# Two unused tiles that shift the matmul operands of a hybrid DeltaNet / mLSTM layer to multiples of 512 bytes

## The chip, the cores and the metric

The kernel runs on one core of one Trainium2 chip. The metric is the time of one execution on the device, in microseconds (us); the median of several runs counts. The core has a tensor engine (TensorE: matmuls, whose stationary operand is loaded beforehand and whose moving operand streams past it), VectorE, ScalarE, GpSimd (POOL) and 16 DMA engines. Work on different engines overlaps as far as data allow. On-chip memory has 128 partitions; a tile occupies the same byte range in each of them, so a tile has one start address, counted in bytes from the beginning of a partition.

## What is computed

One layer of a bidirectional backbone on 128 context tokens and 256 latent tokens, width 2048, all in float32. The two blocks below run once for the context and once for the latents; `mod` comes from `silu(cond) @ w_ada + b_ada`.

```python
def block(x, mod, init_states, lp, grid):
    ...
    shift1, scale1, gate1, shift2, scale2, gate2 = jnp.split(mod, 6, axis=-1)
    h = rmsnorm(x, pre1) * (1.0 + scale1) + shift1
    mix, states = mixer(h, grid, init_states, w_in, conv_w, a_log, dt_bias, norm_a, ibias, fbias, norm_b, w_out)
    x = x + gate1 * rmsnorm(mix, post1)
    h = rmsnorm(x, pre2) * (1.0 + scale2) + shift2
    f = jnp.square(jax.nn.relu(h @ w1)) @ w2
    x = x + gate2 * rmsnorm(f, post2)
    return x, states
```

`mixer` projects `h` with `w_in` (2048 x 7216), runs a gated delta rule (8 heads) and an mLSTM (4 heads) forward and backward in chunks, and projects the joined heads with `w_out` (2048 x 2048). The feed-forward part has a hidden width of 8192.

## The kernel before

All 384 tokens (three tiles of 128) are worked on together. Every large product has a right-hand side of weights from HBM. A weight block of two k-tiles (128 x 2 x 512 floats, 512 KB) lands in a tile `raw`; ScalarE rounds it to the reduced float format that TensorE takes at full rate (`whi`, line 332) and VectorE computes what is left (`wlo`, line 333). The activations are held in two such parts as well, so that each product is done as three: high by low, high by high, low by high. `gemm` writes these triples in two forms. With `fm` true (lines 356 to 358), the weights are stationary and 384 tokens move: the projections of q, k and v and the up projection of the feed-forward part. With `fm` false (lines 360 to 362), 128 tokens are stationary and 512 weight columns move: the projections of the mLSTM values and gates, the output projection (`mid`, activations `y`) and the down projection (`ffn`, activations `ah` and `al`). For the last weight blocks of the output and of the down projection (`room`), the weights are held in tiles of their own (`w_ah`, `w_al`, and `w` in the memory of `h`).

The order of the stages is: set-up and `phase1` (normed input, modulation, mLSTM projections), the mLSTM heads, four quarters of the delta rule (whose own small products stand between the triples of the next projection), the output projection with residual and second norm (`mid`), the feed-forward part (`ffn`: eight chunks, the up projection of one ahead of the down projection of the one before), and the last norm. Steps of the modulation (`ps_ada`, line 190, and `adav` on VectorE, line 220) are put between the large products by `fill`. Each engine takes its instructions in the order in which they are written, with some parts moved forward by a priority.

Tiles are allocated in pools, and pools that live at the same time lie behind one another: first `cp` (constants), then `hp` (activation operands `h`, `y`), `wp` (`raw`, `whi`, `wlo`), `wk` (small work tiles), and behind these the pools of the stage, of which `fp` is the one of `mid` and `ffn`. A tile's start is therefore the sum of what lies ahead of it. In the built program, all tiles of `hp` and `wp` begin at 160 bytes past a multiple of 512, and the large ones of `fp` at 480 past one. Slices that the products take (a k-tile of 1536 or 2048 bytes, a block of 128 columns of 512 bytes) keep that remainder.

Of the kernel before, what the change touches and what calls it, by code (L numbers as in the profile page):

```python
# [12 lines left out]
F32 = mybir.dt.float32  # L13
# [8 lines left out]
P = 128  # L22
# [114 lines left out]


def ada_mod(S, sec, k0, m, pv):
    """Bias of the modulation columns pv [P, m, 2], and what each section is used as: shift, scale or gate."""  # L140
    nc, c = S.nc, S.c
    i = sec // 3
    cols = lambda t, o: t[:, o + k0:o + k0 + m].unsqueeze(2).to_broadcast([P, m, 2])
    bias = cols(c.pcol, 16 * sec)
    if sec % 3 == 0:
        nc.vector.tensor_tensor(c.tcol[i][:, k0:k0 + m, :], pv, bias, op=ALU.add)
        return
    tmp = S.wk.tile([P, m, 2], F32, tag="adatmp", name="adatmp")
    nc.vector.tensor_tensor(tmp, pv, bias, op=ALU.add)
    if sec % 3 == 1:  # L150
        nc.vector.scalar_tensor_tensor(c.scol[i][:, k0:k0 + m, :], in0=tmp, scalar=1.0, in1=cols(c.pcol, 96 + 16 * i),
                                       op0=ALU.add, op1=ALU.mult)
    else:
        nc.vector.tensor_tensor(c.gcol[i][:, :, k0:k0 + m].rearrange("p v k -> p k v"), tmp,
                                cols(c.pcol, P + 16 * i), op=ALU.mult)


def ada_cols(S, ps, n):
    """Four groups of 32 rows of sums, n wide, turned into columns: [P, group, block, row of the group]."""
    nc = S.nc  # L160
    row = S.wk.tile([P, 256], F32, tag="modrow", name="modrow", bufs=1)
    nc.scalar.copy(row[:, 0:n], ps[:, 0:n])
    pt = S.pa.tile([P, 512], F32, tag="a", name="ps_col")
    for i in range(n // P):
        nc.tensor.transpose(pt[:, i * P:i * P + P], row[:, i * P:i * P + P], S.c.ident)
    t = S.wk.tile([P, 4, n // P, 2], F32, tag="modcol", name="modcol")
    nc.vector.tensor_copy(t, pt[:, 0:n].rearrange("p (i j r) -> p j i r", j=4, r=32)[:, :, :, 0:2])
    return t


def ada_steps(S, units, n):
    """Blocks of n columns of silu(cond) @ w_ada + b_ada, units (section, first column), brought to columns; one step
    at a time, to go between the steps of a larger product. Four products at a time, each on its own 32 columns of
    the tensor engine: the units, and as many k-tiles as there is room for."""
    nc, c = S.nc, S.c
    nu = len(units)
    npar = 4 // nu
    kn = 1024 // (nu * n)
    ps = S.pa.tile([P, 512], F32, tag="a", name="ps_ada")
    for k in range(0, NK, kn):  # L180
        raw = S.wp.tile([P, kn, nu * n], F32, tag="raw", name="raw_ada", bufs=S.nraw)
        runs = [(0, nu)] if nu == 4 else [(u, u + 1) for u in range(nu)]
        for u, e in runs:
            o = units[u][0] * D + units[u][1]
            nc.sync.dma_start(raw[:, :, u * n:e * n], S.A.w_ada[0, k * P:(k + kn) * P, o:o + (e - u) * n]
                              .rearrange("(k p) n -> p k n", p=P))
        for kk in range(kn):
            for u in range(nu):
                j = u * npar + (k + kk) % npar
                nc.tensor.matmul(ps[32 * j:32 * j + 32, 0:n], lhsT=c.scz[:, k + kk, :],  # L190
                                 rhs=raw[:, kk, u * n:u * n + n], start=k + kk < npar, stop=k + kk >= NK - npar)
        yield
    t = ada_cols(S, ps, n)
    m = n // P
    if npar == 1:
        ada_mod(S, units[0][0], units[0][1] // P, 4 * m, t.rearrange("p j i v -> p (j i) v"))
        return
    for u, (sec, c0) in enumerate(units):
        s = S.wk.tile([P, m, 2], F32, tag="modsum", name="modsum")
        nc.vector.tensor_tensor(s, t[:, 2 * u], t[:, 2 * u + 1], op=ALU.add)  # L200
        ada_mod(S, sec, c0 // P, m, s)


def ada_vec(S, sec, c0):
    """The same for 512 columns of a section, summed over the k-tiles by the vector engine."""
    nc, c = S.nc, S.c
    while S.av is None:
        yield
# [24 lines left out]


def fill(S, n=None):
    """Some steps of the work that waits to go between the steps of the products."""
    if n is None:
        S.credit += S.rate
        n = int(S.credit)
# [13 lines left out]


def ada_later(S, sec, nvec=0):
    """A section by halves of 1024 columns on the tensor engine, the last nvec by the vector engine."""
    for i in range(2):
        if i < 2 - nvec:
            S.todo.append(ada_steps(S, [(sec, 1024 * i + 256 * u) for u in range(4)], 256))
# [7 lines left out]


def gate_rows(S, i):
    """gate * post-norm weight as rows in DRAM, to be broadcast over the tokens."""  # L270
    nc, c = S.nc, S.c
    ps = S.pa.tile([P, 512], F32, tag="a", name="ps_gr")
    nc.tensor.transpose(ps[0:32, 0:P], c.gcol[i].rearrange("p v k -> p (v k)"), c.ident)
# [12 lines left out]


def build_hT(S, xs, kt, which, diag=None):
    """h^T of one 128-feature block (all tokens), split in two float32r parts."""
    nc, c = S.nc, S.c  # L290
    ps = S.pm.tile([P, 512], F32, tag="m", name="ps_hT")
    for t in range(NT):
# [12 lines left out]


def diag_of(S, r, t):
    """diag(r): transposes and scales rows in one product."""
    d = S.wk.tile([P, P], F32, tag="diag", name="diag", bufs=3)
    S.nc.vector.tensor_scalar(d, S.c.ident, r, None, op0=ALU.mult)  # L310
    return d


def alloc_act(S):
    """Two halves of an activation operand [2048, 384] as float32r pairs."""
    hh = [[S.hp.tile([P, 8, TOK], F32R, tag=f"h{a}{b}", name=f"h{a}{b}") for b in range(2)] for a in range(2)]
    return lambda kt: (hh[kt // 8][0][:, kt % 8, :], hh[kt // 8][1][:, kt % 8, :])


def wchunk(S, srcs, kn, dst=None):  # L320
    """kn k-tiles of a block of weights, side by side from srcs, as a float32r pair whose sum is exact."""
    nc = S.nc
    n = sum(ap.shape[1] for ap in srcs)
    raw = S.wp.tile([P, kn, n], F32, tag="raw", name="raw", bufs=S.nraw)
# [10 lines left out]


def gemm(S, fm, wsrc, kcs, act, evac, psum=None, kn=2, between=None, room=()):
    """A block of act^T W over chunks kcs of kn k-tiles; fm: features on partitions, otherwise tokens. With room for
    the weights of the last chunks, these are held and multiplied with one tile of tokens after the other, so that
    what follows a tile need not wait for the rest."""  # L340
    nc = S.nc
    psum = psum or (lambda s: S.pg.tile([P, 512], F32, tag="g", name="ps_g"))
    ps = [None] * 4
# [41 lines left out]


def phase1(S):
    """x, modulation and the mLSTM projections, by quarters of the contraction."""
    nc, tc, A, c = S.nc, S.tc, S.A, S.c
    S.hT = alloc_act(S)  # L390
    S.bqk = [S.mp.tile([P, 2, TOK], F32, tag=f"bqk{h}", name=f"bqk{h}") for h in range(HB)]
# [74 lines left out]


def setup3(S, p1):
    """The gate columns of w_in, padded to a width that the tensor engine takes in one pass, in two parts."""
    nc, A = S.nc, S.A  # L470
    w = p1.tile([P, NK, GW], F32, name="wg")
    nc.gpsimd.memset(w, 0.0)
# [17 lines left out]


def rows3(S, nat, n, name):
    """n per-token columns as rows over the tokens, each the exact sum of three bfloat16 rows 32 apart: a one-hot
    column then spreads a row over all partitions in one pass."""
    nc = S.nc
    pad = S.ga.tile([P, NT, 80], F32, name=name + "p")
    nc.vector.memset(pad, 0.0)
# [17 lines left out]


def gates(S, gt):
    """Per-token gate scalars of both mixers, tokens on partitions."""
    nc, c, gp = S.nc, S.c, S.gp
    G = S.G = SimpleNamespace()  # L520
    T = lambda n, name: gp.tile([P, NT, n], F32, name=name)
# [227 lines left out]
        nc.gpsimd.memset(t, 0.0)  # L749


# Diagonal 32 x 32 blocks between rows on partitions, [(block, row), unit, col], and blocks on partitions,
# [(block, unit), row, col]: with 13 units, prime to 32, both are one regular walk over the DRAM tile.
NI = 52  # L754
DMA_SCRATCH = 1024
LAY = 32 * 13 * 4 * 32 + 32 * 13 * 32
# [25 lines left out]


def delta_quarter(S, q, sqk, sv):
    """Gated delta rule of heads 2q and 2q + 1, both directions."""
    Q = SimpleNamespace()
    Q.qT = [sqk[:, h, :] for h in range(2)]
    Q.kT = [sqk[:, 2 + h, :] for h in range(2)]
# [82 lines left out]


def delta_sub(S, Q):
    """Inverses of the 32 x 32 diagonal blocks, one block per partition, by forward substitution."""
    nc, dl, Am = S.nc, S.dl, Q.Am
    dA, dX = [S.dr.tile([LAY], F32, tag=f"dA{i}", name=f"dA{i}") for i in range(2)]
    tA, X = S.tA, S.X
# [16 lines left out]


def delta_levels(S, Q):
    """The diagonal blocks joined to the inverse of the whole 128 x 128 triangle."""
    nc, dl, Am, pt, dX = S.nc, S.dl, Q.Am, Q.pt, Q.dX
    Tm, Nc = S.Tm, S.Nc
    Nx = dl.tile([P, 13, 32], F32, tag="Nx", name="Nx", bufs=1)  # L900
# [50 lines left out]


def delta_scan(S, Q, q):
    """The tiles in order, for two heads and two directions in step."""
    nc, c, G = S.nc, S.c, S.G
    kT, col, pt, w, at, qe, nk, sv = Q.kT, Q.col, Q.pt, Q.w, Q.at, Q.qe, Q.nk, Q.sv
    chains = [(d, h) for d in range(2) for h in range(2)]
# [85 lines left out]


def ag_block(S, n):
    """Gates of four delta heads; then the gated, normed outputs, transposed and split."""
    nc, c = S.nc, S.c
    ga = S.de.tile([P, NT, 512], F32, tag="slq", name="ga", bufs=2)

# [15 lines left out]


def mid(S):
    """Output projection, first residual, second norm and modulation."""
    nc, tc, A, c = S.nc, S.tc, S.A, S.c
    S.x1 = [S.fp.tile([P, D], F32, name=f"x1_{t}") for t in range(NT)]  # L1070
    mp = S.fp
# [9 lines left out]
        nc.vector.tensor_tensor(S.x1[s][:, cs], ps, gp1[min(s, 1)][:, cs], op=ALU.mult)  # L1081

    def load(n, i):
        """Rows that the residual needs, between the weights."""
        if i in (4, 5):
            cs = slice(n * 512, n * 512 + 512)
            nc.sync.dma_start(gp1[i - 4][:, cs], S.gpd[0][i - 4][cs].partition_broadcast(P))
# [119 lines left out]
def body(tc, A, O):  # L1207
    with ExitStack() as ctx:
# [10 lines left out]
        S.pg = ent(tc.tile_pool(name="pg", bufs=4, space=PSUM))  # L1219
        S.pm = ent(tc.tile_pool(name="pm", bufs=3, space=PSUM))  # L1220
        S.pa = ent(tc.tile_pool(name="pa", bufs=1, space=PSUM))
        S.gpd = [S.drp.tile([2, D], F32, name=f"gpd{i}") for i in range(2)]
        S.gbd = [S.drp.tile([P, 1024], F32, name=f"gbd{t}") for t in range(NT)]
        with ExitStack() as mx:
# [38 lines left out]
            yA_finish(S, 1, g1)  # L1263
        S.fp = ent(tc.tile_pool(name="fp", bufs=1, reuse_waits="tile"))
        S.av = S.fp
        S.rate = R2
        mid(S)
        S.rate = R3
# [20 lines left out]
```

## Time and profile before

| what | value |
|---|---|
| median of three runs | 2026.45 us (2025.23 to 2031.12) |
| span of the profiled execution (its own time, first to last instruction) | 2022.6 us |
| TensorE busy | 1960.9 us, 97% |
| VectorE busy | 1166.6 us, 58% |
| ScalarE busy | 710.8 us, 35% |
| moved from and to HBM | 166 GB/s over the span |

The profile is one execution. PE stands for TensorE's matmuls, PEld for its loads of stationary operands, which overlap them; DVE is VectorE and ACT is ScalarE. Matmuls are pipelined: a product's duration reaches past the start of the next one, so the pace of a stream of products is the distance from start to start, and not the duration of one. A busy share of 97% says that TensorE seldom waits, and not that it works at its peak.

### The profile page before, as it was taken

The page shows a single profiled execution, that of the slowest core. Times are in us where ns is not written, and L with a number is a line of the kernel's source. Part 1 is how long each engine was busy: PE and PEld are TensorE (multiplying, and loading weights), DVE is VectorE, ACT ScalarE, POOL GpSimd, SP SyncE. Part 2 cuts the span into 40 slices and gives each one's busy share as a digit, 9 for nine tenths or more (in the row PEclk, how much of TensorE's full clock was granted, in tenths as well). Part 3 has the DMA queues.
Part 4 walks back from the last instruction along what each step waited for, and adds up shares of the span by engine and source line. Part 5 has one row for each costly group of instructions (what it writes and reads, how often), then busy time and mean ns, then how long its engine had stood idle before and what let it go on. Part 6 is the DMA issues. An engine that isn't in the chain of part 4 may idle for free.

```text
span 2022.6 us, 28836 instructions
## 1 busy us (share of the span) xinstructions
PE 1960.9 (97%) x11332; PEld 1672.3 (83%) x11332; DVE 1166.6 (58%) x2144; ACT 710.8 (35%) x1125; POOL 123.0 (6%) x125
## 2 busy tenths in 40 slices
PE   6999997999999999998999999999999999999997
PEld 4677886788888777788998897988988989889886
DVE  3766883668878766767554465556543343343445
ACT  5222242444444334335433342332332423323322
POOL 2000000010000000000100010000000100000002
PEclk9999998999999999999999999999999999999999
DMA  9988448776576566762454554555544434444452
GB/s 271 293 265 263 126 127 145 165 190 200 164 196 186 154 197 202 266 205 74 142 161 156 165 158 150 161 155 160 157 135 125 127 126 127 129 126 127 125 167 104
DMA packets 232356, 337.25 MB, mean 167 GB/s; under 512 B 46272, under 2 KB 115584, under 8 KB 231196
## 3 DMA queue, kind: packets, MB, share of 16 engines
q1 hardware_dynamic: 214120, 333.15, 55.1%
q10 hardware_dynamic: 17620, 2.11, 0.7%
q8 instruction: 89, 1.46, 0.3%
q14 instruction: 47, 0.39, 0.1%
q0 software_dynamic: 480, 0.15, 0.0%
HBM read 326.80 MB, written 8.56 MB: 166 GB/s over the span
## 4 chain that ended last, share of the span: by engine, by line
PE 72%; DVE 2%; DMA 1%; ACT 0%; issue 0%; POOL 0%; DVEq 0%; POOLq 0%; ACTq 0%
PE ps_g L356 11%; PE ps_g L358 10%; PE ps_g L357 10%; PE ps_dn L362 9%; PE ps_dn L360 9%; PE ps_dn L361 9%; PE ps_g L360 3%; PE ps_g L362 3%; PE ps_g L361 3%; PE ps_ada L190 2%; PE ps_o L1027 1%; DVE wlo L333 1%; PE ps_z L993 1%; DMA raw_av<-w_ada 1%; PE ps_S L1006 0%; PE ps_ks L984 0%
## 5 line engine op out<-in xcount | busy, mean ns | idle before, releaser
L333 DVE TENSOR_TENSOR wlo<-raw,whi 128x1024 fp32r<-128x1024 f32 (+1 forms) x402 | 487.1, 1212 | 586.8 <-ACT whi L332 585.8
L332 ACT CAST whi<-raw 128x1024 fp32r<-128x1024 f32 (+1 forms) x402 | 416.8, 1037 | 1029.5 <-PE ps_g L357 380.6
L356 PE MATMUL ps_g<-h,whi 128*128 128x384 f32 x1536 | 522.7, 340 | 0.5 <-DVE cv L737 0.5
L358 PE MATMUL ps_g<-h,wlo 128*128 128x384 f32 x1536 | 516.3, 337 | 2.1 <-DVE wlo L333 2.1
L357 PE MATMUL ps_g<-h,whi 128*128 128x384 f32 x1536 | 516.8, 336 | 0.0
L356 PEld LDWEIGHTS ps_g<-h,whi 128*128 128x128 f32 x1536 | 288.8, 188 | 20.7 <-issue 18.6
L362 PE MATMUL ps_dn<-wlo,ah 128*128 128x512 f32 x756 | 298.3, 395 | 1.0 <-DVE wlo L333 1.0
L360 PE MATMUL ps_dn<-whi,al 128*128 128x512 f32 x756 | 298.7, 395 | 0.0
L361 PE MATMUL ps_dn<-whi,ah 128*128 128x512 f32 x756 | 298.4, 395 | 0.0
L358 PEld LDWEIGHTS ps_g<-h,wlo 128*128 128x128 f32 x1536 | 288.5, 188 | 5.0 <-DVE wlo L333 4.0
L357 PEld LDWEIGHTS ps_g<-h,whi 128*128 128x128 f32 x1536 | 288.8, 188 | 1.1 <-issue 0.4
L362 PEld LDWEIGHTS ps_dn<-wlo,ah 128*128 128x128 f32 x756 | 141.6, 187 | 36.5 <-DVE wlo L333 1.8
L360 PEld LDWEIGHTS ps_dn<-whi,al 128*128 128x128 f32 x756 | 141.6, 187 | 36.0 <-issue 1.6
L361 PEld LDWEIGHTS ps_dn<-whi,ah 128*128 128x128 f32 x756 | 141.6, 187 | 34.0
L220 DVE SCALAR_TENSOR_TENSOR adav<-raw_av,scz,adav 128x512 f32<-128x512 f32 x180 | 130.6, 774 | 13.0 <-DMA raw_av<-w_ada 12.8
L1148 POOL TENSOR_TENSOR rl<-rl 128x384 f32<-128x384 f32 x64 | 68.1, 1073 | 886.6 <-ACT ah L1147 886.4
L360 PE MATMUL ps_g<-whi,h 128*128 128x512 f32 x288 | 118.4, 411 | 0.5 <-ACT whi L332 0.4
L361 PE MATMUL ps_g<-whi,h 128*128 128x512 f32 x288 | 114.6, 398 | 0.0
L362 PE MATMUL ps_g<-wlo,h 128*128 128x512 f32 x288 | 113.6, 398 | 0.2 <-DVE wlo L333 0.2
L190 PE MATMUL ps_ada<-raw_ada,scz 128*32 128x256 f32 (+1 forms) x1216 | 102.0, 389 | 5.0 <-DMA raw_ada<-w_ada 3.4
L190 PEld LDWEIGHTS ps_ada<-raw_ada,scz 128*32 128x32 f32 x1216 | 34.1, 113 | 47.7 <-issue 27.4
L360 PEld LDWEIGHTS ps_g<-whi,h 128*128 128x128 f32 x288 | 54.1, 188 | 23.1 <-issue 11.3
(400 smaller groups left out, 1899.1 us busy)
## 6 DMA issues: line engine op xcount, KB each, us to landing
raw<-w_ffn SPq DMA_DIRECT2D x256, 512.0 KB, 3.8
raw_ada<-w_ada SPq DMA_DIRECT2D x80, 512.0 KB, 5.0
raw<-w_in SPq DMA_DIRECT2D x74, 512.0 KB, 4.4
raw_ada<-w_ada SPq DMA_DIRECT2D x128, 256.0 KB, 4.8
raw_av<-w_ada SPq DMA_DIRECT2D x48, 512.0 KB, 4.6
raw<-w_in SPq DMA_DIRECT2D x76, 256.0 KB, 3.1
raw<-w_out SPq DMA_DIRECT2D x32, 512.0 KB, 4.6
x<-x_sample SPq DMA_DIRECT2D x2, 1024.0 KB, 9.8
```

Of the source, the lines that this page charges most:

```text
L190: nc.tensor.matmul(ps[32 * j:32 * j + 32, 0:n], lhsT=c.scz[:, k + kk, :], rhs=raw[:, kk, u * n:u * n + n], start=k + kk < npar, stop=k + k ...
L220: nc.vector.scalar_tensor_tensor(acc[:, v, :], in0=raw[:, kt % 2, :], scalar=w, in1=acc[:, v, :], op0=ALU.mult, op1=ALU.add)
L332: nc.scalar.copy(hi, raw)
L333: nc.vector.tensor_tensor(lo, raw, hi.bitcast(F32), op=ALU.subtract)
L356: nc.tensor.matmul(o, lhsT=hi[:, kk, w], rhs=al, start=st, stop=False)
L357: nc.tensor.matmul(o, lhsT=hi[:, kk, w], rhs=ah, start=False, stop=False)
L358: nc.tensor.matmul(o, lhsT=lo[:, kk, w], rhs=ah, start=False, stop=sp)
L360: nc.tensor.matmul(o, lhsT=al[:, w], rhs=hi[:, kk, :], start=st, stop=False)
L361: nc.tensor.matmul(o, lhsT=ah[:, w], rhs=hi[:, kk, :], start=False, stop=False)
L362: nc.tensor.matmul(o, lhsT=ah[:, w], rhs=lo[:, kk, :], start=False, stop=sp)
L993: nc.tensor.matmul(pz[:, i * P:(i + 1) * P], lhsT=S.Tm[d][:, 3 * h + tof(d), :], rhs=r[d, h], start=True, stop=True)
L1148: nc.gpsimd.tensor_tensor(rl, rl, rl, op=ALU.mult)
```

## The change

Two tiles are allocated that nothing writes or reads: 88 floats (352 bytes of a partition) as the first tile of `cp`, and 48 floats (192 bytes) as the first of `fp`. Besides, the comment lines at the head of some functions are gone.

```diff
@@ body
         S.pa = ent(tc.tile_pool(name="pa", bufs=1, space=PSUM))
+        S.cp.tile([P, 88], F32, name="padc")
         S.gpd = [S.drp.tile([2, D], F32, name=f"gpd{i}") for i in range(2)]
...
         S.av = S.fp
+        S.fp.tile([P, 48], F32, name="padf")
         S.rate = R2
```

The built programs have the same instructions, in the same order on every engine and with the same waits. The starts of the tiles (bytes past a multiple of 512) are:

| pool, tiles | before | after |
|---|---|---|
| `hp`: `h`, `y`, `w` | 160 | 0 |
| `wp`: `raw`, `whi`, `wlo` | 160 | 0 |
| `fp`: `x1`, `y2`, `gp1`, `gp2`, `ah`, `al`, `w_ah`, `w_al` | 480 | 0 |
| `fp`: `rl` / `adav`, `fj` | 128 / 32 | 160 / 64 |
| `mp`: `bqk` / `vaug` | 128 / 128, 160, 192 | 480 / 480, 0, 32 |
| delta rule: `da` / `slq`, `slv`, `cv` / `Am`, `DT`, `qe` / `Tm` | 128 / 0 / 384 / 192 | 480 / 352 / 224 / 32 |
| `p1`: `x`, `bo`, `wgh` | 352, 384, 384 | 192, 224, 224 |

## Rows read from the trace of the kernel before

**Rows 1.** The page's head and busy times: us (share of the span) xinstructions.

```profile
span 2022.6 us, 28836 instructions
...
PE 1960.9 (97%) x11332; PEld 1672.3 (83%) x11332; DVE 1166.6 (58%) x2144; ACT 710.8 (35%) x1125; POOL 123.0 (6%) x125
```

**Rows 2.** Windows by stage, us: busy time of each engine (instructions), granted clock, DMA.

```profile
core 0: us, PE busy (x) PEld busy (x) DVE busy (x) ACT busy (x) POOL busy (x), PEclk, DMA share, GB/s
0.00:120.00 120.00, 100.02 (x717) 70.30 (x721) 66.57 (x145) 42.05 (x64) 14.45 (x27) 1.00 0.92 279
120.00:280.00 160.00, 159.71 (x936) 130.00 (x929) 120.52 (x226) 43.91 (x54) 0.00 (x0) 1.00 0.62 193
280.00:420.00 140.00, 122.04 (x679) 99.71 (x678) 79.30 (x247) 63.93 (x140) 6.19 (x9) 0.94 0.76 150
420.00:770.00 350.00, 347.94 (x2845) 284.62 (x2844) 258.00 (x741) 145.32 (x339) 15.03 (x8) 1.00 0.63 184
770.00:917.00 147.00, 145.73 (x692) 114.50 (x690) 103.83 (x155) 55.24 (x81) 1.10 (x2) 1.00 0.68 226
917.00:930.00 13.00, 5.56 (x25) 4.80 (x25) 9.40 (x22) 9.70 (x15) 2.12 (x4) 0.74 0.24 81
930.00:1068.00 138.00, 137.35 (x806) 136.64 (x806) 81.17 (x111) 53.48 (x76) 14.04 (x14) 1.00 0.46 138
1068.00:2013.00 945.00, 942.54 (x4651) 831.70 (x4650) 443.43 (x494) 296.48 (x360) 69.50 (x62) 1.00 0.46 140
```

**Rows 3.** Waits of TensorE: waiting for whom, us in total, times, longest.

```profile
PE ps_c L94 <- ACT crs L93: 8.5, 1, 8.5
...
PE ps_ada L190 <- DMA raw_ada<-w_ada: 3.4, 3, 2.9
...
PE ps_num L689 <- ACT cf L676: 15.8, 3, 8.0
...
PE ps_hT L295 <- DVE s L1118: 7.0, 1, 7.0
```

**Rows 4.** One line in one up projection, 1677 to 1744 us: durations, first and last start.

```profile
L357 PE MATMUL ps_g<-h,whi x128: 334/334/338, 1677.3 to 1743.4; 128*128 128x384 f32 x128
```

**Rows 5.** Timeline of TensorE in the output projection: start us, duration us.

```profile
859.81 0.39 PE L360 MATMUL ps_g<-whi,y 128*128 128x512 f32 x1
...
861.85 0.39 PE L360 MATMUL ps_g<-whi,y 128*128 128x512 f32 x1
```

**Rows 6.** One line in one down projection, 1744 to 1811 us.

```profile
L361 PE MATMUL ps_dn<-whi,ah x96: 394/394/394, 1744.0 to 1810.5; 128*128 128x512 f32 x96
```

**Rows 7.** A window without other work, and TensorE's timeline in it.

```profile
2000.00:2002.20 2.20, 2.20 (x11) 1.75 (x10) 0.00 (x0) 0.00 (x0) 0.00 (x0) 1.00 0.00 0
...
1999.81 0.39 PE L362 MATMUL ps_dn<-w,ah 128*128 128x512 f32 x1
...
2002.14 0.39 PE L360 MATMUL ps_dn<-whi,al 128*128 128x512 f32 x1
```

**Rows 8.** Plain float32 products of an mLSTM head: timeline, and durations of that line.

```profile
382.45 1.03 PE L689 MATMUL ps_num<-vaug,E 128*128 128x257 f32 x4
...
L689 PE MATMUL ps_num<-vaug,E x8: 377/379/380, 381.6 to 384.0; 128*128 128x257 f32 x8
```

**Rows 9.** Groups by line and shape: count, busy us, mean ns, idle before.

```profile
L356 PE MATMUL ps_g<-h,whi 128*128 128x384 f32 x1536 | 522.7, 340 | 0.5 <-DVE cv L737 0.5
...
L360 PE MATMUL ps_dn<-whi,al 128*128 128x512 f32 x756 | 298.7, 395 | 0.0
...
L360 PE MATMUL ps_g<-whi,h 128*128 128x512 f32 x288 | 118.4, 411 | 0.5 <-ACT whi L332 0.4
L360 PE MATMUL ps_g<-whi,y 128*128 128x512 f32 x180 | 71.4, 397 | 0.0
...
L360 PE MATMUL ps_dn<-w,al 128*128 128x512 f32 x12 | 4.7, 396 | 0.0
L360 PE MATMUL ps_g<-w_ah,y 128*128 128x512 f32 x6 | 2.4, 396 | 0.0
```

**Rows 10.** The same groups: the first of the delta rule's products of 128 columns.

```profile
L1027 PE MATMUL ps_o<-vv,at 128*128 128x128 f32 x96 | 17.6, 278 | 0.0
```

**Rows 11.** The page's groups: the split of the weights.

```profile
L333 DVE TENSOR_TENSOR wlo<-raw,whi 128x1024 fp32r<-128x1024 f32 (+1 forms) x402 | 487.1, 1212 | 586.8 <-ACT whi L332 585.8
L332 ACT CAST whi<-raw 128x1024 fp32r<-128x1024 f32 (+1 forms) x402 | 416.8, 1037 | 1029.5 <-PE ps_g L357 380.6
```

## The prediction

> **What bounds the kernel now.** I read the page's first lines, then the windows by stage, then who waits for whom, and last the spacing of the large products. The profiled execution spans 2022.6 us and TensorE is busy in 1960.9 us of it [rows 1]; the median of the three timed runs is 2026.45 us, so 3.9 us lie around the span and are added to every forecast. By stage TensorE is busy nearly without a gap from 120 us to the end, save the gate and mLSTM stretch (122.0 of 140 us) and the hand-over to the feed-forward part (5.6 of 13 us) [rows 2]. What TensorE waited for is short: 8.5 us for ScalarE at the start, 15.8 us for the mLSTM states, 7.0 us at the hand-over, 3.4 us for weights from DMA [rows 3]. In the feed-forward stretch, 945 us, VectorE is busy for 443 and ScalarE for 296 us and DMA at 0.46 [rows 2]. So the end is set by how fast TensorE takes one large product after the other, and the question is whether the start of a tile has a say in that.
>
> TensorE's granted clock is 1.00 there [rows 2], the 2.4 GHz level, at which 512 columns are 213.3 ns and 384 columns 160.0 ns. The products with 384 moving columns follow each other in 66.1 us / 127 / 3 = 173.5 ns (three lines in turn, the middle one 128 times from 1677.3 to 1743.4 us) [rows 4]: 13.5 ns over their columns. The output projection's, 512 columns, do nine steps in 2.04 us, 226.7 ns: 13.4 ns over [rows 5]. The down projection's, also 512 columns, take 66.5 us / 95 / 3 = 233.3 ns: 20.0 ns over [rows 6]. Between 2000.0 and 2002.2 us nothing else runs (VectorE, ScalarE and DMA all at zero), and there too ten steps take 2.33 us, 233 ns [rows 7], so neighbours' traffic is not the cause. Same shape, same clock, two speeds. What differs is where the operands begin. In the output projection both do at 160 bytes past a multiple of 512; in the down projection the moving tile at 160 and the stationary `ah`/`al` at 480. The plain float32 products of the mLSTM, with moving tiles `vaug` that begin at 128, 160 and 192, take (1.03 - 0.38) / 3 = 217 ns for 257 columns [rows 8]; that is 2.5 ns over two times 257 columns at 2.4 GHz, so they read at half the rate and show hardly any excess whatever their start.
>
> **The change part by part.** It adds two tiles that nobody writes or reads. No instruction is added or removed, and on no engine does one move or gain a wait, so nothing is costed there. What changes is addresses alone.
>
> First, the operands of all large products go to a start of 0. They are 1536 x 3 = 4608 products of 384 columns, (288 + 180) x 3 + 36 = 1440 of 512 columns at the 226.7 ns level, and 756 x 3 + 36 = 2304 at the 233.3 ns level [rows 9] (each printed row stands for three lines, the two held-weight rows for 36 products each). No product in this trace has both operands at 0, so the price is bounded. The upper end of the gain is that all excess goes: 4608 x 13.5 + 1440 x 13.4 + 2304 x 20.0 ns = 62.2 + 19.3 + 46.1 = 127.6 us. The lower end, if starts matter at all, is that the down projection falls to the level of the output projection and the others stay: 2304 x 6.6 ns = 15.2 us. I take a value near the upper end, with the 2.5 ns of the plain products [rows 8] left over: 4608 x 11.0 + 1440 x 10.9 + 2304 x 17.5 = 50.7 + 15.7 + 40.3 = 106.7 us of TensorE time. The reason is the form of the excess: 13.4 and 13.5 ns for 512 and 384 columns is a fixed sum, no share of the columns. It is 32 columns at 2.4 GHz, or 128 bytes of a row, as if one piece more were read; a row that begins inside a piece touches one piece more, a row that begins on its edge does not. The products that read at half the rate have time to hide it.
>
> Not all of it reaches the end. From 770 us on (output projection, 576 products, and the feed-forward part, 3072 and 2304) TensorE never waits long and the gain counts in full: 3072 x 11.0 + 576 x 10.9 + 2304 x 17.5 = 33.8 + 6.3 + 40.3 = 80.4 us. Before 770 us the other 1536 products of 384 and 864 of 512 columns hold 16.9 + 9.4 = 26.3 us. I count half, 13 us: in the first 120 us DMA is busy at 0.92, in the mLSTM stretch TensorE already idles for 18 us, and between 420 and 770 us VectorE is busy for 258 of 350 us [rows 2], so a faster TensorE meets others' chains. Sum: 93 us.
>
> Second, the other pools shift by the same 352 bytes. The delta mixer's tiles leave multiples of 128 for 96 past one. If plain float32 products with 128 columns then paid the 13.5 ns, 480 of them (ten rows like the first printed) would cost 6.5 us [rows 10]; by the `vaug` products I count nothing. VectorE and ScalarE read and write the shifted tiles too, but their work lies under TensorE's, with 502 us to spare on VectorE in the feed-forward stretch [rows 2]. What is late next there is the weight split: a pair of k-tiles is 18 products, 4.2 us now and 3.9 us then, against 1.04 us on ScalarE and 1.21 us on VectorE [rows 11], so it stays hidden. The 3.4 us of DMA waits [rows 3] stay.
>
> **The rivals.** *Only the mismatch costs.* The excess may come from the two reads of a product getting in each other's way, by the distance of their starts: 0 bytes apart in the output projection, 320 in the down projection. Then the change mends the down projection alone: 2026.5 - 15.2 = 2011 us. For it speaks that both slow and fast products have a moving tile at 160; against it that a distance of 0 still has 13.4 ns of excess.
>
> *The start has no say.* The two levels may belong to the region of memory (the projection's `y` lies below 58 KB of a partition, `ah`/`al` above 126 KB), and the 13.4 ns to this kind of product. Then the time stays at 2026 us. For it: no row has an aligned start. Against it: nothing in the trace names a region as such. The Trainium skill ("SBUF — State Buffer", Specifications) knows lines of 16 bytes, at full speed for neighbouring accesses. Both 160 and 480 are multiples of 16, so by that rule the change would do nothing, and by the same rule the two levels should not exist; here the trace does not agree with it.
>
> *Equal starts collide.* With everything at a multiple of 512, weights and moving rows begin on the same edge; if that is the bad case, the 6048 products that are at the lower level rise by one such step of 6.6 ns, 40 us, and the down projection stays: 2066 us. It decides as soon as the steady spacing of 384 columns exceeds 173.5 ns. Against it: the output projection has equal starts already, at 160, and is the faster.
>
> **How the numbers follow.** The likeliest case: 2022.6 - 93 = 1929.6 us of span, 1933.5 us with what lies around it. Chance 0.50, by itself from 1905 us (127.6 us gained, nearly in full) to 1970 us (half of the excess gone). Only the mismatch, 2011 us: 0.18. No say, 2026 us: 0.19. Collision, 2066 us: 0.13. A range from 1908 to 2031 us holds the first three cases and leaves out the last and the first one's edge, in all below 2 in 10. The runs lie within 0.3% of each other, 6 us, which is about what a measurement can tell. Faster by more: the first two cases, 0.68. Same: 0.19. Slower: 0.13.
>
> **What would show it.** Right, if the middle line of the up projection runs its 128 products in about 61.9 us instead of 66.1 (162.5 ns a step), and the down projection's 96 in about 61.5 us instead of 66.5 (215.8 ns); if the gain sits in the feed-forward stretch; and if TensorE's idle time grows by some 13 us before 770 us. Wrong, if the spacing of 384 columns stays at 173.5 ns: then the fixed excess is not one piece more read, and at most 15 us are to be had. Wrong in the sum alone, if the spacing falls as said and VectorE or the weights' DMA begin to hold TensorE up.

## The result and the profile after

The median fell from 2025.84 us (2023.27 to 2031.12, 4 runs) to 2005.32 us (2002.55 to 2008.65, 4 runs): a ratio of 0.9896, with a 95% interval of 0.9883 to 0.9909, so 1.0% or some 21 us less. The profiled execution's own time is 2004.86 us, its span 2003.1 us. The direction was forecast, the size was not: 93 us were expected.

The page's head and busy times of the changed kernel, against [rows 1]:

```profile
span 2003.1 us, 28836 instructions
...
PE 1944.5 (97%) x11332; PEld 1673.4 (84%) x11332; DVE 1166.2 (58%) x2144; ACT 711.1 (35%) x1125; POOL 122.8 (6%) x125
```

The same instructions, and on every engine but TensorE the same busy time; TensorE's fell by 16.4 us. Next, the middle line of one up projection, lines of the output projection, and the middle line of one down projection, against [rows 4 to 6]:

```profile
L357 PE MATMUL ps_g<-h,whi x128: 334/334/338, 1663.0 to 1729.1; 128*128 128x384 f32 x128
```

```profile
850.14 0.39 PE L360 MATMUL ps_g<-whi,y 128*128 128x512 f32 x1
...
852.18 0.39 PE L360 MATMUL ps_g<-whi,y 128*128 128x512 f32 x1
```

```profile
L361 PE MATMUL ps_dn<-whi,ah x96: 389/389/397, 1729.7 to 1794.3; 128*128 128x512 f32 x96
```

The up projection still takes 66.1 us / 127 / 3 = 173.5 ns a product, the output projection 2.04 us / 9 = 226.7 ns. Only the down projection fell, from 233.3 to 64.6 us / 95 / 3 = 226.7 ns. A start at 0 is thus no better than one at 160; what went is the distance between the two levels. The first and the last start of the two outer lines give the stage as a whole, before and after:

```profile
L360 PE MATMUL ps_dn<-whi,al x756: 388/394/505, 1068.2 to 2009.1; 128*128 128x512 f32 x189
...
L362 PE MATMUL ps_dn<-w,ah x12: 390/396/398, 1999.8 to 2012.4; 128*128 128x512 f32 x12
```

```profile
L360 PE MATMUL ps_dn<-whi,al x756: 387/389/499, 1062.9 to 1989.5; 128*128 128x512 f32 x189
...
L362 PE MATMUL ps_dn<-w,ah x12: 388/389/393, 1980.4 to 1992.7; 128*128 128x512 f32 x12
```

From the first to the last of these products 944.2 us became 929.8 us: 14.4 of the 19.5 us between the two spans. The other 5 us were gained before these products, nearly all of it in the mLSTM stretch, where the wait of 15.8 us [rows 3] is shorter:

```profile
PE ps_num L689 <- ACT cf L676: 10.9, 3, 7.4
```

### The profile page after: what moved, and what is told of

The parts are those of the page before. It is cut to its first block, busy times and chain, and to the rows that moved or that the text cites. A ratio compares the mean times of both kernels' runs of the same rounds, so it can differ in the third digit from the quotient of the medians.

```text
span 2003.1 us, 28836 instructions
## 1 busy us (share of the span) xinstructions
PE 1944.5 (97%) x11332; PEld 1673.4 (84%) x11332; DVE 1166.2 (58%) x2144; ACT 711.1 (35%) x1125; POOL 122.8 (6%) x125
## 4 chain that ended last, share of the span: by engine, by line
PE 89%; DMA 5%; DVE 4%; ACT 1%; issue 1%; POOL 0%; SPq 0%; ACTq 0%; DVEq 0%; POOLq 0%
PE ps_g L356 13%; PE ps_g L358 13%; PE ps_g L357 12%; PE ps_dn L360 8%; PE ps_dn L362 8%; PE ps_dn L361 8%; PE ps_g L360 5%; PE ps_g L362 5%; PE ps_g L361 5%; PE ps_ada L190 4%; DMA raw<-w_in 2%; DVE wlo L333 1%; PE ps_o L1027 1%; DMA raw_av<-w_ada 1%; PE ps_num L689 1%
## 5 line engine op out<-in xcount | busy, mean ns | idle before, releaser
L360 PEld LDWEIGHTS ps_g<-whi,h 128*128 128x128 f32 x288 | 54.5, 189 | 24.2 <-issue 11.7
```

What stands on the lines that cost most here:

```text
L360: nc.tensor.matmul(o, lhsT=al[:, w], rhs=hi[:, kk, :], start=st, stop=False)
```

## The experiments

All starts are bytes past a multiple of 512; a "mark" is the start of `ah` and `al`, and a triple is the three products of lines 360 to 362; a "row" is what a product reads of an operand in one partition. The theories and rivals that are named by letters stand in the expectations. The triple's time is worked out from the rows of the middle line: last start less first start, by 95 steps.

**Each spare tile alone.** The first run drops the second tile, the second run the first:

```diff
-        S.fp.tile([P, 48], F32, name="padf")
```

> Only the first spare tile: h, y and the weight tiles begin at 0, ah/al and the held weights at 320 past a multiple of 512. Theory A (only the difference of the two starts of a product counts): the difference of the down projection is 320 as before, so its spacing stays at 233.3 ns, the other products at 173.5 and 226.7 ns, and the time is 15 us above that of the full change, about 2020 us. Theory B (it is the stationary tile's own start that counts, and 480 is a bad one, for instance because it is no multiple of 64): 320 is a multiple of 64, the down projection falls to 226.7 ns, and the time is that of the full change, 2005 us.

```diff
-        S.cp.tile([P, 88], F32, name="padc")
```

> Only the second spare tile: all operands of the large products begin at 160 past a multiple of 512. Theory A (difference): 226.7 ns in the down projection, 2005 to 2011 us; the 5 us beyond the down projection, won in the mLSTM stretch, would be lacking if they come from the first tile. Theory B (own start; multiples of 64 or of 512 are needed): 160 is neither, so the down projection stays at 233.3 ns and the time at 2026 us.

The first tile alone: 2022.95 us, ratio 0.9987 (0.9976 to 0.9997). The second alone: 2011.23 us, ratio 0.9930 (0.9915 to 0.9946). The middle line of one down projection in each:

```profile
L361 PE MATMUL ps_dn<-whi,ah x96: 394/394/394, 1742.4 to 1808.9; 128*128 128x512 f32 x96
```

```profile
L361 PE MATMUL ps_dn<-whi,ah x96: 389/389/397, 1731.9 to 1796.5; 128*128 128x512 f32 x96
```

66.5 us and 64.6 us, a triple of 700 and of 680 ns. With everything at 160 the down projection is as fast as with everything at 0, and with its stationary operand at a multiple of 64 that differs from the moving one's start it is as slow as before. Theory A holds here and theory B falls. The second run also says something on the mLSTM wait: up to the output projection this kernel is the one before, address by address, and yet

```profile
PE ps_num L689 <- ACT cf L676: 12.5, 3, 7.2
```

So that wait varies from execution to execution; in the other runs of this study with float32r operands it was 11.1 to 13.6 us, and the 15.8 us of [rows 3] were a long one. The start of the output projection says the same, in the kernel before, in the changed kernel and in a later run with the changed kernel's addresses up to there (the ruler at 192 and 448):

```profile
L360 PE MATMUL ps_g<-whi,y x180: 389/389/499, 775.1 to 913.6; 128*128 128x512 f32 x180
```

```profile
L360 PE MATMUL ps_g<-whi,y x180: 389/389/499, 769.4 to 907.8; 128*128 128x512 f32 x180
```

```profile
L360 PE MATMUL ps_g<-whi,y x180: 388/389/499, 776.6 to 915.8; 128*128 128x512 f32 x180
```

The ten runs with these addresses (the first tile alone, the rulers, the rows of 384 columns) came there at 770.1 to 776.6 us, this run with the old ones at 771.1 us. The 5 us between the two profiles are thus within what executions with the same addresses differ by, and show no effect of the addresses. The medians leave room for a small one: by itself the first tile brings 0.13%, just clear of no change, and the interval of the second tile alone (from 0.9915) lies above that of both together (to 0.9909).

**Unequal starts elsewhere.** The first spare tile is put in `wp`, so that `h` and `y` stay at 160 while the weights begin at 0; in a second run the weights, `ah` and `al` begin at 480.

```diff
         S.wp = ent(tc.tile_pool(name="wp", bufs=2))
+        S.wp.tile([P, 88], F32, name="padc", bufs=1)
...
-        S.cp.tile([P, 88], F32, name="padc")
```

> h and y begin at 160, the weight tiles and ah/al at 0. Theory A (difference): now the two operands of phase 1, the up projection and the output projection differ by 160, so 4608 products of 384 columns rise from 173.5 to about 180 ns and 1440 of 512 from 226.7 to 233.3 ns, about 40 us in all, 2045 us, and the down projection stays at 226.7 ns. Theory B (own start): h at 160 was fast in the kernel before and the weights at 0 are fast in the changed one, so nothing changes, 2005 us.

```diff
+        S.wp.tile([P, 80], F32, name="padw", bufs=1)
...
-        S.cp.tile([P, 88], F32, name="padc")
```

> h and y begin at 160, weights, held weights and ah/al at 480. The down projection has equal starts at 480, the mark of ah/al in the kernel before: by theory A 226.7 ns, by a bad own start of 480 (theory B) 233.3 ns. The up projection has its stationary operand 320 past its moving one, the difference that cost the down projection most: by theory W about 174 ns, by a price that follows the difference alone 180 ns (4608 x 6.6 = 30 us more). Phase 1 and the output projection lie at 231 to 235 ns, some 1440 x 6.6 = 10 us. Sum by A and W 2015 us, by the price alone 2045 us.

Measured: 2015.1 us, ratio 0.9946 (0.9933 to 0.9959), and 2023.71 us, ratio 0.9982 (0.9970 to 0.9993). The output projection's timeline and the up projection's middle line in the first of the two:

```profile
859.68 0.39 PE L360 MATMUL ps_g<-whi,y 128*128 128x512 f32 x1
...
862.48 0.39 PE L360 MATMUL ps_g<-whi,y 128*128 128x512 f32 x1
```

```profile
L357 PE MATMUL ps_g<-h,whi x128: 336/336/337, 1806.1 to 1872.2; 128*128 128x384 f32 x128
```

and the up and the down projection's in the second:

```profile
L357 PE MATMUL ps_g<-h,whi x128: 338/338/338, 1806.8 to 1874.1; 128*128 128x384 f32 x128
```

```profile
L361 PE MATMUL ps_dn<-whi,ah x96: 389/389/389, 1741.6 to 1806.2; 128*128 128x512 f32 x96
```

With a stationary operand 160 past the moving one, the output projection took 2.80 us / 12 = 233.3 ns: the price of the down projection, brought about in another place. With both at 480 the down projection took 680 ns a triple, so 480 is no bad mark. But the up projection (384 columns) paid less: 66.1 us for its 128 products in the first run, nothing more than before, and 67.3 us / 127 / 3 = 176.6 ns in the second, 3.1 ns for a difference that costs 512 columns 6.6 ns. Theory A in its plain form asked 40 and 30 us here, and that failed. Theory W, with about 174 ns and 2015 us for the second run, was too low as well: 3.1 ns in each of 4608 such products are 14 us.

**Does the length of the row count, or the side?** The kernel with the first spare tile alone, rows cut to 384 columns.

```diff
...
-                nc.tensor.matmul(o, lhsT=ah[:, w], rhs=hi[:, kk, :], start=False, stop=False)
...
+                n0 = 384 if cut else 512
+                nc.tensor.matmul(o[:, 0:n0], lhsT=ah[:, w], rhs=hi[:, kk, 0:n0], start=False, stop=False)
...
```

> The kernel with the first spare tile alone (stationary ah/al at 320, weights at 0, where the down projection took 233.3 ns), its moving rows cut to 384 of 512 columns in all but the first and the last product of a sum (a quarter of the output columns gets a wrong sum). Theory W (the price of unequal starts depends on the length of the moving row, and 384 columns pay next to none, as the up projection at a difference of 160): the spacing is 173.5 to 174.5 ns. Rival R (it depends on which operand is which: weights as stationary operand pay none): 384 columns pay the same 6.6 ns here, 180 ns.

The run took 1905.9 us. In the timeline of its down projection, nine products of 384 columns, and the middle line of that projection:

```profile
1689.95 0.34 PE L362 MATMUL ps_dn<-whi,al 128*128 128x384 f32 x1
...
1691.53 0.33 PE L362 MATMUL ps_dn<-whi,al 128*128 128x384 f32 x1
```

```profile
L364 PE MATMUL ps_dn<-whi,ah x96: 333/338/339, 1668.7 to 1719.8; 128*128 128x384 f32 x96
```

1.58 us / 9 = 175.6 ns. Over the whole projection it is 174.8 ns: 51.1 us less 22 products of 512 columns at 233.3 ns, shared by 263 products of 384. That is 1.3 to 2.1 ns over the 173.5 ns at equal starts, where 512 columns pay 6.6: the price does depend on the length (theory W), and rival R, with 180 ns, falls. The side may count a little besides, since the same rest of 64 bytes cost the up projection 3.1 ns. Why a shorter row pays less is not settled.

**A ruler.** `ah` and `al` have two buffers each, used by even and odd chunks. Columns added to the tiles, and another size of the second spare tile, give them marks of their own against weights at 0.

```diff
-        hi = fp.tile([P, 8, TOK], F32R, tag="ah", name="ah", bufs=2)
-        lo = fp.tile([P, 8, TOK], F32R, tag="al", name="al", bufs=2)
+        hi = fp.tile([P, 8 * TOK + 8], F32R, tag="ah", name="ah", bufs=2)
+        lo = fp.tile([P, 8 * TOK + 16], F32R, tag="al", name="al", bufs=2)
+        hi, lo = [x[:, 0:8 * TOK].rearrange("p (k n) -> p k n", n=TOK) for x in (hi, lo)]
```

> The changed kernel with ah and al at starts of their own in even and odd chunks: ah at 0 and 32, al at 64 and 128, the weights at 0. Theory A in its plain form (every difference costs): only the products after which ah at 0 is loaded (even chunks, from line 360 to 361 and from 361 to 362) keep 226.7 ns, those of 32, 64 and 128 take 233.3 ns. Theory A with a period (a difference that is a multiple of 64, or of 128, is none): 64 and 128, or 128 alone, keep 226.7 ns, and 32 takes 233.3 ns. Theory B (own start, multiples of 64 are good): 32 alone takes 233.3 ns.

> The ruler at other marks: ah at 192 and 256 past a multiple of 512, al at 320 and 384, weights at 0. Theory A in the form that the first ruler left (no period of 64 or 128; every difference costs, a small one less): all intervals of the down projection lie between 229 and 235 ns, the time is near that of the first ruler and above it, 2017 to 2022 us. Rival (a period of 256 bytes): ah at 256 in odd chunks keeps 227 ns from line 361 to 362.

> The ruler at the far marks: ah at 416 and 448 (96 and 64 before the next multiple of 512), al at 480 and 96. Theory A, if the difference counts to the nearest multiple of 512: 480 and 448 are 32 and 64 away and cost as little as 32 and 64 did (229.5 and about 231 ns). Theory A, if it counts in one direction only: 416, 448 and 480 cost as much as 320 did, 233.3 ns.

> The ruler at the middle marks: ah at 160 and 224, al at 288 and 352. With it all multiples of 32 have been tried once. Theory A: no mark but 0 gives 227 ns; 160 gives what the output projection showed at that difference, about 231 ns, and 288 and 352 what 320 gave, 233 ns. Rival (a product can be had below 226.7 ns at some difference, so that the fixed excess of 13.4 ns is a matter of the difference too): some mark shows an interval below 226 ns.

> The ruler with ah and al at the same mark: 0 in even chunks, 256 in odd ones. The four rulers gave 693.1 to 694.4 ns for the three products of a triple where ah and al stood at different marks, 699.1 and 699.9 where 320 was among them, and 680.4 with all at 0. Theory A with one price for one difference: the odd chunks give 699 to 700 ns as 320 did, the even ones 680 ns, about 2012 us. Rival (256 is a half period and costs less): the odd chunks give below 693 ns.

> The ruler with ah and al at the same mark, 64 in even chunks and 320 in odd ones. If the rule has a period of 256 bytes, both are the same difference, and both give 700 ns for a triple as 320 did, about 2025 us. If only 256 itself is an exception (or the period is none), 64 gives another sum than 320, for instance 693 ns as in the first ruler where 64 and 0 were mixed.

> The ruler with ah and al at the same mark, 192 in even chunks and 448 in odd ones. With a period of 256, both give the 687 ns that the output projection showed at 192 past (stationary at 160, moving at 480), about 2010 us. Without it, 448 differs from 192, and the plain form of theory A (one price for every difference) gives 700 ns.

> The ruler with ah and al at the same mark, 128 in even chunks and 384 in odd ones. With a period of 256 both give the same sum for a triple; the marks 64, 160 and 192 gave 700, 700 and 687 ns, so it should lie between 687 and 700 ns, and not at 680 ns, which would make the period 128.

Single times were 2017.18, 2022.77, 2019.15, 2019.32, 2010.11, 2021.96, 2016.97 and 2017.76 us. The middle line in one even and one odd chunk of the last four:

```profile
L361 PE MATMUL ps_dn<-whi,ah x96: 389/389/397, 1603.1 to 1667.7; 128*128 128x512 f32 x96
...
L361 PE MATMUL ps_dn<-whi,ah x96: 389/389/397, 1735.0 to 1799.6; 128*128 128x512 f32 x96
```

```profile
L361 PE MATMUL ps_dn<-whi,ah x96: 394/394/394, 1607.8 to 1674.3; 128*128 128x512 f32 x96
...
L361 PE MATMUL ps_dn<-whi,ah x96: 394/394/394, 1741.6 to 1808.1; 128*128 128x512 f32 x96
```

```profile
L361 PE MATMUL ps_dn<-whi,ah x96: 394/394/394, 1607.6 to 1672.8; 128*128 128x512 f32 x96
...
L361 PE MATMUL ps_dn<-whi,ah x96: 394/394/394, 1740.1 to 1805.3; 128*128 128x512 f32 x96
```

```profile
L361 PE MATMUL ps_dn<-whi,ah x96: 390/393/404, 1604.7 to 1670.9; 128*128 128x512 f32 x96
...
L361 PE MATMUL ps_dn<-whi,ah x96: 390/393/404, 1738.2 to 1804.4; 128*128 128x512 f32 x96
```

| `ah` and `al` at | one down projection, us | a triple, ns |
|---|---|---|
| 0, 256 | 64.6, 64.6 | 680 |
| 64, 320 | 66.5, 66.5 | 700 |
| 128, 384 | 66.2, 66.2 | 697 |
| 192, 448 | 65.2, 65.2 | 686 |
| 0 / 64, 32 / 128 (first ruler) | 65.9, 65.9 | 694 |
| 192 / 320, 256 / 384 (second) | 66.6, 65.9 | 701, 694 |
| 416 / 96, 448 / 480 (third) | 65.9, 65.8 | 694, 693 |
| 160 / 288, 224 / 352 (fourth) | 65.8, 65.9 | 693, 694 |

Marks 256 apart are one and the same mark: the difference counts by its rest to 256 bytes. A rest of 0 costs nothing, 64 costs 20 ns a triple, 128 17 ns and 192 6 ns; the output projection above, at 160, paid 20 ns. The plain form of theory A (one price for any difference) fell with 256 and 192, the rival with a period of 64 or 128 too. Where `ah` and `al` differ from one another a triple lies at about 694 ns whatever the marks, save with 320 in it; in the first ruler's even chunks, some 380 steps of each kind, it was the two beside the product with `al` at 64 that took 234 and 232 ns on average (lines 360 to 361 and 362 to 360), while the third kept 227. So one unequal operand in three slows two steps of three. The price of mixed marks is not a sum of single prices: 192 with 320 gave 701 ns, where 192 alone gives 686 and 320 alone 700. How they combine is open. No mark gave a triple below 680 ns, so the 13.4 ns are no matter of the difference.

**What the 13.4 ns belong to.** First the load of the stationary operand, cut to half as many columns in two products of a triple, and then in all three:

```diff
...
+                if half:
+                    o, w = ps[s][0:64], slice(s * P, s * P + 64)
                 nc.tensor.matmul(o, lhsT=ah[:, w], rhs=hi[:, kk, :], start=False, stop=False)
...
```

> The changed kernel, with only 64 of the 128 token columns as stationary operand in the second and third product of each triple of the down projection; half of their output rows are left out. The moving rows are as long as before. Theory L (the 13.4 ns by which a product exceeds its 512 columns are the part of loading the next stationary operand that is not hidden): intervals next to a load of 64 columns fall to about 220 ns, in two of three, 2 x 756 x 6.7 ns = 10 us less, 1995 us. Rival M (the excess belongs to the moving rows, whatever is loaded, as the prediction had it with one piece of a row more): all intervals stay at 226.7 ns and the time at 2005 us.

```diff
...
-        w = slice(s * P, s * P + P)
+        w = slice(s * P, s * P + (64 if half else P))
...
```

> The changed kernel with 64 of the 128 token columns as stationary operand in every product of the down projection (half of its output rows are left out and set to zero), so that no load of 64 columns stands beside one of 128. If the 13.4 ns over the 512 columns are the reading of the next stationary operand, taken from the moving rows (theory L), they halve: 220 ns, and the time falls by 2268 x 6.7 = 15 us to 1990 us. If they belong to the moving rows or to the product as such (rival M), 226.7 ns stay, 2005 us. If a load of 64 columns is done in a slower way than one of 128 (rival S, for which the run with mixed loads speaks), the spacing rises above 227.9 ns, to 233 ns or more.

2013.83 us and 2014.82 us in one run each: both slower than the four runs of the changed kernel. The middle line of the first; that of the second, and above it the loads of its stationary operand; then the changed kernel's loads:

```profile
L364 PE MATMUL ps_dn<-whi,ah x96: 388/393/398, 1736.6 to 1802.0; 128*64 128x512 f32 x96
```

```profile
L362 PEld LDWEIGHTS ps_dn<-whi,ah x96: 133/134/135, 1737.0 to 1802.5; 128*64 128x64 f32 x96
L362 PE MATMUL ps_dn<-whi,ah x96: 389/393/398, 1737.2 to 1802.8; 128*64 128x512 f32 x96
```

```profile
L361 PEld LDWEIGHTS ps_dn<-whi,ah x96: 187/188/188, 1729.4 to 1794.1; 128*128 128x128 f32 x96
```

A load fell from 188 to 134 ns, and a product rose from 226.7 to 65.6 us / 95 / 3 = 230.2 ns (65.4 us and 229.5 ns in the first run). Loading less buys nothing, which rules out theory L in the form that it had here. Rival S got the sign and missed the size; rival M missed by 3.5 ns. Then the type of the operands: whole bfloat16 tiles, and bfloat16 read in place from the four-byte values.

```diff
...
-        hi = fp.tile([P, 8, TOK], F32R, tag="ah", name="ah", bufs=2)
...
+        hi = fp.tile([P, 8, TOK], BF16, tag="ah", name="ah", bufs=2)
...
```

> The changed kernel with the high and low parts of the down projection's operands as bfloat16 tiles instead of float32r (same tiles, starts, shapes and number of products; two bytes for each value in place of four, and less precise sums). If the 13.4 ns go with four-byte operands read at the full rate, which leave no room for reading the next stationary operand (theory L in the form: bytes), they fall to the 2.5 ns that other products show: 215.8 ns, 2268 x 10.9 = 25 us less, 1980 us. If they belong to every product that loads a stationary operand beside it (rival M), 226.7 ns and 2005 us stay.

```diff
...
+                    ah, al = ah.bitcast(BF16), al.bitcast(BF16)
+                    rh, rl = [x[:, kk, :].bitcast(BF16)[:, 1::2] for x in (hi, lo)]
...
```

> The changed kernel, the down projection's products reading the upper two bytes of each float32r value in place, as bfloat16 with a step of two (the values are cut, so the sums are less precise). The rows reach over as many bytes as with float32r. If the excess goes with the bytes that a row reaches over, 226.7 ns stay as in the changed kernel; if it goes with the type of the operands, the spacing is that of the run with whole bfloat16 tiles.

1985.91 us and 2004.22 us. Timelines of a down projection in the first and in the second, six steps each, and behind either the loads of its middle line:

```profile
1739.63 0.38 PE L362 MATMUL ps_dn<-whi,ah 128*128 128x512 bf16 x1
...
1740.93 0.38 PE L362 MATMUL ps_dn<-whi,ah 128*128 128x512 bf16 x1
```

```profile
L362 PEld LDWEIGHTS <-ah x96: 97/98/102, 1719.3 to 1780.9; 128*128 128x128 bf16 x96
```

```profile
1739.79 0.39 PE L367 MATMUL ps_dn<-whi,al 128*128 128x512 bf16 x1
...
1741.14 0.39 PE L367 MATMUL ps_dn<-whi,al 128*128 128x512 bf16 x1
```

```profile
L368 PEld LDWEIGHTS <-ah x96: 96/96/104, 1730.3 to 1794.5; 128*128 128x128 bf16 x96
```

1.30 us / 6 = 217 ns in whole tiles (over all such triples 647.5 / 3 = 215.8 ns), 1.35 us / 6 = 225 ns in place. With the same type, the same columns and nearly the same loads (98 and 96 ns), operands whose values stand four bytes apart keep 11.7 of the 13.4 ns; values two bytes apart keep 2.5 ns. That excludes the load's length and the start, and it speaks for the four bytes from one value to the next and against the type. The excess does not grow with the bytes of a moving row: 384 and 512 float32r columns, 1536 and 2048 bytes, have the same excess. Two things stay open. Both operands changed together, so these runs do not tell whether the moving or the stationary one makes the difference. And the reading in place brought a step of two, which may have a price of its own; then the type could still be what float32r pays for. Last, all large products in bfloat16 parts:

```diff
-F32R = mybir.dt.float32r
+F32R = mybir.dt.bfloat16
...
```

> The changed kernel with all operands of the large products in two bfloat16 parts in place of two float32r parts (same starts and number of products, sums less precise). Theory L (the excess goes with the bytes that TensorE reads): the up projection falls from 173.5 to 162.5 ns a product, the 512-column products to 215.8 ns. From 770 us on that is the 33.8 + 6.3 + 25 = 65 us that the prediction counted there (the down projection from 226.7 now), and of the 26 us before 770 us the half, 13 us, if the prediction's guess on others' chains is right: 2005 - 78 = 1927 us; 1914 us if the early part counts in full too. Rival M (the fall in the down projection was one of its own): 1986 us.

1932.29 us (1929.26 to 1938.34, 4 runs), ratio to the kernel before 0.9536 (0.9508 to 0.9563), the fastest of the kernels here that leave no column out, with sums that are less precise than those of the two kernels compared here. Its up projection, the start of its output projection and the end of its down projection:

```profile
L357 PE MATMUL ps_g<-h,whi x128: 326/326/326, 1731.4 to 1793.3; 128*128 128x384 bf16 x128
```

```profile
L360 PE MATMUL ps_g<-whi,y x176: 377/379/390, 757.2 to 890.9; 128*128 128x512 bf16 x176
```

```profile
L362 PE MATMUL ps_dn<-w,ah x11: 379/379/379, 1907.2 to 1918.9; 128*128 128x512 bf16 x11
```

128 products of the up projection in 61.9 us, the 162.5 ns that the prediction had wanted of the new starts. The Trainium skill ("TensorE: Matmul & The Clock Gate", Back-to-back issue gap) gives a gap of the columns at 2.4 GHz and 2.5 ns for a matmul by itself: by that, as an estimate, 162.5 ns for 384 columns and 215.8 ns for 512. The same section of the Trainium skill calls this too long for a stream at large column counts; here the middle of long streams with bfloat16 operands shows just these figures, 162.5 and 215.8 ns, and streams with float32r operands 173.5 and 226.7 ns.

## Why the prediction was wrong

**What bounds the kernel** was right: TensorE's pace from 770 us on sets the end, and what its products gained arrived there.

**The price of a start** is the step that failed. The prediction took the 13.4 ns at 160 and the 20.0 ns of the down projection for one thing, a row that begins inside a piece and so reads one piece more, and chose a value near the upper bound, 106.7 us of TensorE time; TensorE's busy time fell by 16.4 us. They are two things. 6.6 ns come from a difference between the starts of the stationary and the moving operand; they went with equal starts at 160 and at 480 as well as at 0, and came back in the output projection when its starts were made unequal. The 13.4 ns do not hang on a start at all: they stayed at 0, and fell to 2.5 ns when values stood two bytes apart in place of four. The prediction had named the sign itself: the spacing of 384 columns stayed at 173.5 ns. The argument "a fixed sum, no share of the columns" was a right reading, since 384 and 512 columns do have the same excess, but it does not point to the start of a row. That the plain float32 products show no such excess at any start could have been read the other way: there too the rate of reading, not the start, was what differed.

**The lower bound** was the answer: 15.2 us for the down projection alone, measured 14.4 us from its first to its last product. It was the first rival, *only the mismatch costs*, at 2011 us and a chance of 0.18. What was held against it, that a difference of 0 still has 13.4 ns of excess, was no objection, since nothing asked the two to have one cause. The median is 6 us below that rival. The parts timed by themselves are 0.13% and 0.70%, together 17 of the 21 us, and their intervals do not exclude that it is the sum; where the first tile's share comes from was not found.

**What reaches the end** was sized well, as far as the all-bfloat16 run shows, which does take the excess away (and shortens the loads as well). From the first product of the output projection (769.4 us in the changed kernel, 757.2 us here) to the last (1992.7 and 1918.9 us) it gained 1223.3 - 1161.7 = 61.6 us, where the prediction's terms, with the down projection taken from 226.7 ns on, make 33.8 + 6.3 + 25 = 65 us; before that point it gained 12.2 us, where half of 26.3 us was counted. The sum of 93 us was built for a change that takes the excess away; this one does not.

**The other pools** cost nothing that shows: the busy times of the other engines are the same within 1 us, and the weight split stayed hidden. (Of the delta rule's tiles `Tm` leaves 192 for 32; the prediction's "multiples of 128 for 96" holds for the others.)

**The other rivals.** *The start has no say* is refuted by the two runs with one tile each. So is, for these products, what the prediction took from the lines of 16 bytes in the Trainium skill ("SBUF — State Buffer", Specifications), that starts at multiples of 16 are all alike: differences of 64 and 160 bytes are such multiples, and they cost 6.6 ns a product. *Equal starts collide* is refuted by the changed kernel and by the runs with equal starts at 160 and 480: all three have the 226.7 ns.

## What to carry to other kernels

Let the moving and the stationary operand of long float32r products begin at the same rest to 256 bytes; of the common rests that were tried, 0, 160 and 224 (a start of 480), none was better than another, and one spare tile ahead of a pool does it. When two speeds of one shape stand side by side in a trace, the difference between them is what a change of addresses can be shown to be worth, and whatever both have in common needs a reason of its own before it is counted. To find what a fixed excess belongs to, change the bytes, the load and the start one by one, and the two operands one by one, which these runs did not do.

## What was not expected

Three things about these products. The price of unequal starts is not all or nothing, but 20, 17, 20 and 6 ns a triple for rests of 64, 128, 160 and 192 bytes; on rows of 384 columns a rest of 64 costs about a fifth to a half of what it costs on 512. A stationary operand of 64 columns in place of 128 made a stream of float32r products slower (230.2 against 226.7 ns) though its load was shorter. And each float32r product here takes 13.4 ns more than its columns, 6% of 512, and bfloat16 products with values two bytes apart only 2.5 ns; how the reading brings this about is open.
